# Two attentions computed by pairs of heads in a transformer kernel whose order comes from a planner

## The chip, the cores and the metric

The kernel runs on one core of one Trainium2 chip. What counts is the device time of one execution in microseconds (us). The kernel before takes 2182.76 us, the median of three runs (2174.44 to 2184.56).

## The reference, cut to what matters

Two transformer blocks run one after the other on 512 tokens of width 1024, all in fp32. The first has a gated linear attention and a sliding-window attention side by side, and then a mixture of 16,384 single-neuron experts. The second has a differential attention and a stick-breaking attention side by side, and then a gated feed-forward layer. The change touches the two attentions below. Both have eight heads of 64 channels, so that one head fills half of the 128 rows or columns of TensorE's array.

```python
# sliding window: blocks of 128 queries see their own 128 keys and the 128 before; 8 query heads, 2 key/value heads
sc = jnp.einsum('bnqhgd,bnkhd->bnhgqk', qb, kb) - slopes * dist      # masked
m = jnp.maximum(jnp.max(sc, axis=-1, keepdims=True), sink)
p = jnp.exp(sc - m)
p = p / (jnp.sum(p, axis=-1, keepdims=True) + jnp.exp(sink - m))
o = jnp.einsum('bnhgqk,bnkhd->bnqhgd', p, vb)

# stick-breaking: 8 heads
z = jnp.einsum('bqhd,bkhd->bhqk', qb, k) * scale
log_1mb = jnp.where(mask, jax.nn.log_sigmoid(-z), 0.0)
rem = lax.cumsum(log_1mb, axis=3, reverse=True) - log_1mb
a = jnp.where(mask, jnp.exp(jax.nn.log_sigmoid(z) + rem), 0.0)
return jnp.einsum('bhqk,bkhd->bqhd', a, v)
```

## The kernel before

**A planner writes the order.** The kernel is a set of Python generators, one for each piece of work (the weight streams, each attention, the experts). A small model of the machine (`Model`, L70) keeps the time at which each engine comes free and at which each tile is written; `Meter` (L176) wraps each engine and charges every instruction a cost as it is issued; `Weaver.run` (L253) always steps the generator that could start first, plus a handicap that the generator may ask for with `late`. So the order of instructions on every engine is fixed when the program is built, and follows from the charges. A matmul is charged in one place (L200): a fast price for float32r operands of 256 columns and more, otherwise 1.67 ns for a column, with no regard to what stands beside it.

**Phase one** (L1552) holds the modulation, the input projection of the first block (`w_in`), the gated linear attention (`gla`, L727), the sliding-window attention (`swa`, L886), the output projection, and the first of the expert work. `swa` runs over four blocks of 128 queries. In each it takes the two key/value heads one after the other. The four query heads of one key/value head lie in the same 64 partitions, so the four score matmuls of `scores(kv)` (L902) all use the same half of the array's rows; their results go to two PSUM banks named `b_s`. Then come bias and maximum (VectorE), exponentials (ScalarE), the division, a transpose of the weights, and `values(kv)` (L951): one matmul of 512 columns for each block of keys into the 64 partitions of `b_acc` that belong to this key/value head, that is into one half of the array's columns.

`gla` already alternates: its loop over `i` (L800) puts the lower and the upper 64 rows in turn, and its state update puts the lower and the upper 64 columns in turn.

**Phase two** (L1561) computes the experts of the two middle blocks of tokens densely. The experts of blocks 0 and 3 are done by `sparse` (L1213) in all three phases: GpSimd gathers one row of 1024 numbers for each of 128 tokens by an indirect DMA (`row<-peer_u`, `row<-peer_v`), and VectorE takes it in with one instruction. There are 512 such rows, four in flight, and VectorE does them between its other work.

**Phase three** (L2241) is the second block. `attend` (L1709) is called for tokens 0 to 383 (here called group a) and again for tokens 384 to 511 (group b), which can begin only when `sparse` is through (the key `X3`). It starts two generators, `stick` (L1814) and `diff` (L1894). `stream` (L1620) runs all matmuls with weights for group a: input projections, output projection, then the feed-forward layer in four parts (`b_mm<-u,whi`, `b_mm<-u,wlo`, `b_mm<-fh,whi`, `b_mm<-fh,wlo`), and the projections of group b. The feed-forward layer of group b (`last_feed`, L2137) comes last.

`stick` takes the heads one by one. For a head and a group of key blocks, `front` (L1817) computes scores into one of two PSUM banks `b_z` from 64 rows of the array (`b_z<-mix,sk`), ScalarE makes three passes over them, VectorE makes the log terms `L`; `back` (L1851) adds the cumulative sums by matmuls with a triangular matrix (`b_z<-L,tri`, `b_z<-Ss,tri`, `b_z<-hide,identb`, all 128 rows), ScalarE takes the exponential into `sba`, and a matmul with the values fills 64 columns (`b_osb<-sba,sv`). The loop puts the front of the next unit ahead of the back of this one:

```python
yield from front(*units[0])
for i, (h, g) in enumerate(units):
    if i + 1 < len(units):
        ...
        yield from front(*units[i + 1])
    yield from back(h, g)
```

Group a has 16 units (eight heads, two groups of key blocks of 384 columns each), group b has eight (512 columns).

The functions that the change touches stand here, with the line numbers that the profile uses; every record in the profile carries L224, the line of `Meter` that issues the instruction, so work is told apart by the names of tiles.

Of the kernel before, what the change touches and what calls it, by code (L numbers as in the profile page):

```python
# [9 lines left out]
F32 = mybir.dt.float32  # L10
# [59 lines left out]
class Model:  # L70
# [7 lines left out]
    def __init__(self):  # L78
        self.free = dict.fromkeys(self.ENGINES, 0.0)
        self.cells = {}  # L80
        self.slots = {}
        self.count = {}
        self.shapes = {}
        self.busy = []
        self.last = 0.0
        self.table = None
        self.tick = [0, 0.0, 0.0]

# [87 lines left out]
class Meter:  # L176
# [7 lines left out]
    def __getattr__(self, op):  # L184
# [5 lines left out]
        def call(*args, **kw):  # L190
# [97 lines left out]
def _emit(ctx, tc, A, dbg):  # L288
# [597 lines left out]
    def swa(pa):  # L886
        for b in range(4):
# [22 lines left out]
            def largest(kv, pss):  # L910
                hs = slice(4 * kv, 4 * kv + 4)
                s = S[kv] = pa.tile([128, 4, 256], F32, name="ss", bufs=2)
                for j in range(4):
                    h = 4 * kv + j
                    DVE.tensor_tensor_reduce(s[:, j, k0:], pss[j // 2][:, j % 2, k0:], dist[:, k0:], 2.0 ** -(h + 1),
                                             -3.0e38, OP.add, OP.max, mx[:, h:h + 1])
                tt(mx[:, hs], mx[:, hs], sinks[:, hs], OP.max)
                tt(es[:, hs], sinks[:, hs], mx[:, hs], OP.subtract)
                DVE.tensor_scalar(mx[:, hs], mx[:, hs], -1.0, None, op0=OP.mult)

            def exps(kv):
                hs = slice(4 * kv, 4 * kv + 4)
                s = S[kv]
                act(es[:, hs], es[:, hs], AF.Exp)
                for j in range(4):
                    h = 4 * kv + j
                    act(s[:, j, k0:], s[:, j, k0:], AF.Exp, bias=mx[:, h:h + 1], accum_out=sm[:, h:h + 1])

            def scale(kv):
                hs = slice(4 * kv, 4 * kv + 4)  # L930
                s = S[kv]
                tt(sm[:, hs], sm[:, hs], es[:, hs], OP.add)
                DVE.reciprocal(sm[:, hs], sm[:, hs])
                tt(s[:, :, k0:], s[:, :, k0:], sm[:, hs][:, :, None].to_broadcast([128, 4, 128 * nk]), OP.mult)

            def turn(kv):
                s = S.pop(kv)
# [771 lines left out]
    def attend(b0, b1, u, tag, pair):  # L1709
# [104 lines left out]
        def stick():  # L1814
            Z, L, po, later, now = {}, {}, {}, {}, {}
# [537 lines left out]
```

## Time and profile before

| | us |
|---|---|
| median of three runs | 2182.76 |
| the profiled execution | 2181.23 |
| its span, first to last instruction | 2179.5 |
| TensorE busy in it | 1987.3 (91%) |
| VectorE busy in it | 1796.9 (82%) |
| ScalarE busy in it | 964.6 (44%) |
| GpSimd busy in it | 662.3 (30%) |
| granted TensorE clock, mean | 0.963 of full speed |

1.7 us of the profiled execution lie outside its span. An fp32 matmul appears as two records on PE, so two records of 256 columns are one matmul of 256 columns. The end of a record is modelled; starts are measured, and the distance from the start of a run of records to the start of what follows is the safest measure of what the run took.

### The profile page before, as it was taken

The page shows a single profiled execution, that of the slowest core. Times are in us where ns is not written, and L with a number is a line of the kernel's source. Part 1 is how long each engine was busy: PE and PEld are TensorE (multiplying, and loading weights), DVE is VectorE, ACT ScalarE, POOL GpSimd, SP SyncE. Part 2 cuts the span into 40 slices and gives each one's busy share as a digit, 9 for nine tenths or more (in the row PEclk, how much of TensorE's full clock was granted, in tenths as well). Part 3 has the DMA queues.
Part 4 walks back from the last instruction along what each step waited for, and adds up shares of the span by engine and source line. Part 5 has one row for each costly group of instructions (what it writes and reads, how often), then busy time and mean ns, then how long its engine had stood idle before and what let it go on. Part 6 is the DMA issues. An engine that isn't in the chain of part 4 may idle for free.

```text
span 2179.5 us, 33115 instructions
## 1 busy us (share of the span) xinstructions
PE 1987.3 (91%) x11701; PEld 1748.8 (80%) x11701; DVE 1796.9 (82%) x3731; ACT 964.6 (44%) x1802; POOL 662.3 (30%) x523
## 2 busy tenths in 40 slices
PE   2889799698999977999999999789988999999998
PEld 1778677587889865799999898578767999988987
DVE  7845887879999977899898798889899999844587
ACT  1331442212586533444444544455554333445365
POOL 0000223432212234454444243345443655300000
PEclk9899899699999988999999999999999999999999
DMA  9964447898888999999999899878876999953487
GB/s 368 354 213 130 151 131 224 261 352 307 297 303 305 329 330 353 339 393 373 385 352 363 305 401 344 301 265 300 290 237 203 371 374 369 331 165 106 165 309 262
DMA packets 226453, 638.11 MB, mean 293 GB/s; under 512 B 21056, under 2 KB 70608, under 8 KB 226288
## 3 DMA queue, kind: packets, MB, share of 16 engines
q1 hardware_dynamic: 152560, 367.54, 47.7%
q0 software_dynamic: 73728, 268.47, 34.5%
q8 instruction: 92, 1.51, 0.3%
q14 instruction: 73, 0.60, 0.1%
HBM read 611.54 MB, written 24.38 MB: 292 GB/s over the span
## 4 chain that ended last, share of the span: by engine, by line
PE 49%; DVE 21%; DMA 13%; issue 9%; POOL 5%; ACT 2%; SPq 0%; DVEq 0%; POOLq 0%; ACTq 0%
PE b_mm L224 31%; PE b_dacc L224 8%; POOL row L224 5%; PE b_z L224 4%; DMA row<-peer_v,eU 4%; DVE row L224 3%; PE b_w L224 3%; DVE o L224 3%; DVE vacc L224 3%; DMA wraw<-peer_v 3%; DVE wlo L224 2%; DMA row<-w_ada 1%; PE b_osb L224 1%; DMA aR<-act_d 1%; DMA row<-w_up 1%
## 5 line engine op out<-in xcount | busy, mean ns | idle before, releaser
L224 POOL DMA_INDIRECT row<-peer_u,eU x256 | 329.4, 1287 | 784.4 <-DVE row L224 247.9
L224 POOL DMA_INDIRECT row<-peer_v,eU x256 | 330.0, 1289 | 436.4 <-DVE row L224 197.8
L224 PE MATMUL b_mm<-h,whi 128*128 128x256 f32 (+2 forms) x1648 | 332.4, 296 | 2.7 <-ACT whi L224 2.2
L224 DVE SCALAR_TENSOR_TENSOR vacc<-row,dots,vacc 128x1024 f32<-128x1024 f32 x254 | 325.4, 1281 | 6.9 <-DMA row<-peer_v,eU 6.3
L224 PE MATMUL b_mm<-u,whi 128*128 128x384 f32 x1216 | 324.2, 347 | 7.5 <-DVE mix L224 2.9
L224 DVE SCALAR_TENSOR_TENSOR row<-row,h2n 128x1024 f32<-128x1024 f32 x256 | 310.6, 1219 | 8.3 <-DMA row<-peer_u,eU 8.2
L224 PEld LDWEIGHTS b_mm<-h,whi 128*128 128x128 f32 (+1 forms) x1648 | 271.9, 190 | 24.0 <-issue 6.9
L224 PE MATMUL b_mm<-h,wlo 128*128 128x256 f32 (+2 forms) x824 | 242.8, 295 | 13.9 <-DVE wlo L224 13.9
L224 PEld LDWEIGHTS b_mm<-u,whi 128*128 128x128 f32 x1216 | 219.1, 190 | 24.8 <-issue 5.6
L224 ACT ACTIVATE whi<-wraw 128x1024 fp32r<-128x1024 f32 (+3 forms) x129 | 125.3, 972 | 184.4 <-PE b_mm L224 126.9
L224 PE MATMUL b_mm<-u,wlo 128*128 128x384 f32 x608 | 205.3, 338 | 0.4 <-DVE wlo L224 0.4
L224 ACT ACTIVATE vhi<-wraw 128x1024 fp32r<-128x1024 f32 x128 | 135.6, 1061 | 146.3 <-PE b_dacc L224 75.4
L224 PE MATMUL b_dacc<-vhi,ghi 128*128 128x512 f32 x512 | 165.3, 405 | 27.7 <-ACT ghi L224 27.5
L224 PE MATMUL b_mm<-h,uraw 128*128 128x256 f32 x704 | 166.3, 385 | 4.5 <-DMA uraw<-peer_uT 3.1
L224 PEld LDWEIGHTS b_mm<-h,wlo 128*128 128x128 f32 (+1 forms) x824 | 156.4, 190 | 16.0 <-DVE wlo L224 15.0
L224 PE MATMUL b_dacc<-vlo,ghi 128*128 128x512 f32 x512 | 163.0, 400 | 1.4 <-DVE vlo L224 1.4
L224 PE MATMUL b_dacc<-vhi,glo 128*128 128x512 f32 x512 | 160.9, 395 | 0.0
L224 DVE TENSOR_TENSOR vlo<-wraw,vhi 128x1024 fp32r<-128x1024 f32 x128 | 156.3, 1221 | 1.8 <-PE b_dacc L224 1.8
L224 PEld LDWEIGHTS b_mm<-h,uraw 128*128 128x128 f32 x704 | 131.7, 194 | 21.2 <-issue 3.5
L224 DVE TENSOR_TENSOR wlo<-wraw,whi 128x1024 fp32r<-128x1024 f32 (+3 forms) x129 | 143.6, 1114 | 3.1 <-ACT whi L224 2.3
L224 DVE TENSOR_TENSOR wlo<-uraw,whi 128x1024 fp32r<-128x1024 f32 x84 | 103.0, 1226 | 44.9 <-ACT whi L224 44.9
L224 PEld LDWEIGHTS b_dacc<-vhi,ghi 128*128 128x128 f32 x512 | 91.9, 192 | 48.0 <-ACT ghi L224 34.0
(376 smaller groups left out, 3696.2 us busy)
## 6 DMA issues: line engine op xcount, KB each, us to landing
uraw<-peer_uT SPq DMA_DIRECT2D x128, 512.0 KB, 6.7
wraw<-peer_v SPq DMA_DIRECT2D x128, 512.0 KB, 8.2
wraw<-w_in SPq DMA_DIRECT2D x60, 512.0 KB, 6.1
row<-w_ada SPq DMA_DIRECT2D x48, 512.0 KB, 7.5
wraw<-w_peer_q SPq DMA_DIRECT2D x32, 512.0 KB, 6.4
gt<-gate_d SPq DMA_DIRECT2D x16, 1024.0 KB, 12.2
gate_d<-stg SPq DMA_DIRECT2D x16, 896.0 KB, 7.4
row<-w_in SPq DMA_DIRECT2D x24, 512.0 KB, 4.3
```

Of the source, the lines that this page charges most:

```text
L224: return f(*args, **kw)
```

## The change

Three things change. `Meter` prices matmuls anew: bfloat16 operands get the fast price, and a matmul that uses 64 rows or 64 columns is charged 0.01 us if the matmul issued just before it used the other half. `swa` no longer goes by key/value heads: a step `u` takes two query heads of each key/value head, the score matmuls alternate between the halves of the rows (and between the two banks), and `values(u)` alternates between the halves of the columns with 256 columns each. `stick` takes a pair of heads at once: both banks `b_z` hold one pair, fronts and value matmuls alternate between the halves, and the front of the next unit is issued after the back of this one.

```diff
             elif op in ("matmul", "transpose"):
                 n = math.prod(args[2].shape[1:]) if op == "matmul" else 128
-                fast = args[1].dtype == F32R and n >= 256
-                m.run("PE", n * 0.000417 + 0.013 if fast else max(n, 32) * (0.00167 if op == "matmul" else 0.00083) + 0.01, [out],
-                      rest,
-                      rows=args[1].shape[0])
+                fast = args[1].dtype == F32R and n >= 256 or args[1].dtype == BF
+                cost = n * 0.000417 + 0.013 if fast else max(n, 32) * (0.00167 if op == "matmul" else 0.00083) + 0.01
+
+                first = lambda ap: ap.offset // math.prod(list(ap.tensor.shape)[1:])
+                k, c = args[1].shape[0], math.prod(args[1].shape[1:])
+                part = ("rows", first(args[1])) if k == 64 else ("columns", first(out)) if c == 64 else None
+                beside = part and m.part and part[0] == m.part[0] and part[1] != m.part[1]
+                m.part = None if beside else part
+                m.run("PE", 0.01 if beside else cost, [out], rest, rows=args[1].shape[0])
...
-            def scores(kv):
-                r = slice(64 * kv, 64 * kv + 64)
+            def scores(u):
                 pss = [bank("s").rearrange("p (j k) -> p j k", j=2) for _ in range(2)]
-                for j in range(4):
-                    PE.matmul(pss[j // 2][:, j % 2, k0:], qs[r, j, 128 * b:128 * b + 128],
-                              ks[r, 128 * b - 128 + k0:128 * b + 128], start=True, stop=True)
+                for i in range(2):
+                    for kv in range(2):
+                        r = slice(64 * kv, 64 * kv + 64)
+                        PE.matmul(pss[kv][:, i, k0:], qs[r, 2 * u + i, 128 * b:128 * b + 128],
+                                  ks[r, 128 * b - 128 + k0:128 * b + 128], start=True, stop=True)
                 return pss
...
-            def values(kv, pTs):
-                r = slice(64 * kv, 64 * kv + 64)
+            def values(u, pTs):
                 for kb, pT in enumerate(pTs, 2 - nk):
-                    PE.matmul(po[r, :], vs[:, b - 1 + kb, 64 * kv:64 * kv + 64], pT, start=(kb == 2 - nk),
-                              stop=(kb == 1))
+                    for kv in range(2):
+                        PE.matmul(po[64 * kv:64 * kv + 64, 256 * u:256 * u + 256],
+                                  vs[:, b - 1 + kb, 64 * kv:64 * kv + 64], pT[:, 256 * kv:256 * kv + 256],
+                                  start=(kb == 2 - nk), stop=(kb == 1), skip_group_check=True)
...
-            def front(h, g):
-                j, r = h // 2, slice(64 * (h % 2), 64 * (h % 2) + 64)
+            def front(j, g):
                 jbs, w = groups[g]
-                z = Z[h, g] = bank("z")
+                zs = Z[j, g] = [bank("z") for _ in half]
                 for jb in jbs:
                     o, m = offs[jb]
-                    PE.matmul(z[:, o:o + m], sk[r, j, 128 * jb:128 * jb + 128], sq[r, j, q0(jb) - c0:],
-                              start=(jb == jbs[0]), stop=True, skip_group_check=True)
+                    for z, r in zip(zs, half):
+                        PE.matmul(z[:, o:o + m], sk[r, j, 128 * jb:128 * jb + 128], sq[r, j, q0(jb) - c0:],
+                                  start=(jb == jbs[0]), stop=True, skip_group_check=True)
...
-                    PE.matmul(po[j][r, n - m:n], sv[:, jb, 64 * h:64 * h + 64], a[:, o:o + m],
-                              start=(jb == b1 - 1), stop=(jb == 0), skip_group_check=True)
...
+                    for i, r in enumerate(half):
+                        PE.matmul(po[r, n - m:n], sv[:, jb, 128 * j + 64 * i:128 * j + 64 * i + 64],
+                                  as_[i][:, o:o + m], start=(jb == b1 - 1), stop=(jb == 0), skip_group_check=True)
...
-            units = [(h, g) for h in range(8) for g in range(len(groups))]
...
+            for j in range(4):
+                for q in ("sq", "sk", "sv"):
+                    yield need(f"{q}{j}{tag}")
+                for g in range(len(groups)):
+                    yield from front(j, g)
+                    if g == 0:
+                        po = bank("osb")
+                    yield from back(j, g, po)
+                yield from unit_norm(sq[:, j], po[:, :n], col("gsb"), "w", False)
+                W.set(f"stick{j}{tag}")
```

Three places show how the order moves. The first is PE in phase one, the second block of queries of the sliding window: transposes `b_s`, values `b_acc`, and the input projection `b_mm<-h` between them. Before:

```order
L224 MATMUL b_acc<-pTs,vs 64x512 x2
L224 MATMUL b_s<-ident,ss 128x128 x8
L224 MATMUL b_mm<-h_141,whi 128x384 x2
L224 MATMUL b_mm<-h_141,wlo 128x384
L224 MATMUL b_mm<-h_141,whi 128x384 x2
L224 MATMUL b_mm<-h_141,wlo 128x384
L224 MATMUL b_acc<-pTs,vs 64x512 x2
```

And after:

```order
L230 MATMUL b_acc<-pTs,vs 64x256 x4
L230 MATMUL b_s<-ident,ss 128x128 x8
L230 MATMUL b_mm<-h_141,whi 128x384 x2
L230 MATMUL b_mm<-h_141,wlo 128x384
L230 MATMUL b_mm<-h_141,whi 128x384 x2
L230 MATMUL b_mm<-h_141,wlo 128x384
L230 MATMUL b_acc<-pTs,vs 64x256 x4
```

The places stay; two matmuls of 512 columns in one half of the columns have become four of 256 that alternate between the halves.

The second is PE in phase three, stick-breaking of group a: the first values `b_osb` of a head, the fronts `b_z<-mix,sk`, the stream `b_mm<-u` and pieces of the differential attention (`b_w`, `b_odf`). Before:

```order
L224 MATMUL b_w<-dk,mix 128x256 x2
L224 MATMUL b_osb<-sba,sv 64x128
L224 MATMUL b_osb<-sba,sv 64x256
L224 MATMUL b_z<-mix,sk 128x128
L224 MATMUL b_z<-mix,sk 128x256
L224 MATMUL b_mm<-u,whi 128x384 x2
L224 MATMUL b_mm<-u,wlo 128x384
```

And after:

```order
L230 MATMUL b_osb<-sba,sv 64x128 x2
L230 MATMUL b_osb<-sba,sv 64x256 x2
L230 MATMUL b_w<-ident,dp 128x128
L230 MATMUL b_mm<-u,whi 128x384 x2
L230 MATMUL b_mm<-u,wlo 128x384
L230 MATMUL b_mm<-u,whi 128x384 x2
L230 MATMUL b_mm<-u,wlo 128x384
L230 MATMUL b_z<-mix,sk 128x384 x2
```

Before, the values of one head stand next to the scores of another; now both heads of a pair stand together, and the next front follows only after their values.

The third is PE where group b begins: the first `b_mm<-u,row` is the first projection of group b. Before:

```order
L224 MATMUL b_mm<-u,whi 128x384 x2
L224 MATMUL b_mm<-u,wlo 128x384
L224 MATMUL b_mm<-u,row 128x128 x16
L224 MATMUL b_mm<-row,u 128x128 x8
L224 MATMUL b_mm<-u,row 128x128 x8
L224 MATMUL b_z<-mix,sk 128x128 x4
L224 MATMUL b_mm<-u,row 128x128 x8
L224 MATMUL b_z<-mix,sk 128x128 x4
```

And after:

```order
L230 MATMUL b_mm<-fh,whi 128x384 x2
L230 MATMUL b_mm<-fh,wlo 128x384
L230 MATMUL b_mm<-u,row 128x128 x16
L230 MATMUL b_mm<-row,u 128x128 x8
L230 MATMUL b_mm<-u,row 128x128 x8
L230 MATMUL b_z<-mix,sk 128x128 x8
L230 MATMUL b_mm<-u,row 128x128 x8
L230 MATMUL b_mm<-row,u 128x128 x8
```

The stream of group a stands further on when group b begins. Counted over the whole order, 2112 of its matmuls stood ahead of group b's first projection, 201 between that and the matmuls by which `last_feed` takes in the residual, and 39 behind; now 2247, 105 and none. On VectorE, 406 of the 512 rows of `sparse` stood ahead of the last output of the differential attention of group a, and 395 do now; ahead of the first `glo` of the dense experts in phase two it was 134 and is 130, ahead of phase two's end 314 and 311.

## Rows read from the trace of the kernel before

**Rows 1.** The page's first part: busy us, share of the span, instructions.

```profile
span 2179.5 us, 33115 instructions
PE 1987.3 (91%) x11701; PEld 1748.8 (80%) x11701; DVE 1796.9 (82%) x3731; ACT 964.6 (44%) x1802; POOL 662.3 (30%) x523
```

**Rows 2.** Busy us by stage: stretch, its length, each engine, PEclk, DMA share, GB/s.

```profile
243.00:326.00 83.00, 78.92 (x481) 62.37 (x480) 70.45 (x169) 36.19 (x85) 26.78 (x23) 0.96 0.52 174
424.00:780.00 356.00, 337.10 (x1960) 305.51 (x1960) 323.43 (x1168) 177.59 (x426) 94.21 (x86) 0.96 0.89 314
905.00:1408.00 503.00, 497.99 (x3101) 445.17 (x3099) 449.28 (x600) 243.75 (x369) 210.96 (x149) 1.00 0.97 359
1450.00:1645.00 195.00, 183.90 (x958) 146.29 (x957) 176.76 (x333) 104.06 (x221) 98.16 (x78) 0.99 0.82 276
1645.00:1909.00 264.00, 252.89 (x1423) 245.72 (x1422) 244.77 (x304) 101.81 (x149) 127.97 (x101) 0.98 0.89 330
1909.00:2060.00 151.00, 148.63 (x1064) 134.71 (x1063) 71.96 (x159) 66.65 (x160) 0.00 (x0) 1.00 0.45 142
2060.00:2180.00 120.00, 108.46 (x726) 97.98 (x724) 86.62 (x92) 75.16 (x89) 0.00 (x0) 0.99 0.80 278
```

**Rows 3.** PE by line, 75 to 330 us: count, busy us, mean ns, idle before.

```profile
L224 PE MATMUL b_s<-ks,yT 64*128 64x256 f32 (+1 forms) x64 | 15.2, 380 | 0.0
L224 PE MATMUL b_acc<-pTs,vs 128*64 128x512 f32 x28 | 13.8, 609 | 0.0
```

**Rows 4.** PE by line, 1450 to 1645 us.

```profile
L224 PE MATMUL b_z<-mix,sk 64*128 64x128 f32 (+2 forms) x48 | 14.6, 411 | 0.0
L224 PE MATMUL b_osb<-sba,sv 128*64 128x128 f32 (+2 forms) x48 | 13.8, 396 | 0.3 <-ACT sba L224 0.2
```

**Rows 5.** PE by line, 1909 to 2060 us.

```profile
L224 PE MATMUL b_z<-mix,sk 64*128 64x128 f32 x64 | 9.2, 285 | 0.0
L224 PE MATMUL b_osb<-sba,sv 128*64 128x128 f32 x64 | 8.7, 279 | 0.0
```

**Rows 6.** PE's timeline at four places: start us, us until the last end, work.

```profile
100.20 0.71 PE L224 MATMUL b_w<-M 64*128 64x128 f32 x8
100.84 1.07 PE L224 MATMUL b_acc<-pTs,vs 128*64 128x512 f32 x2
...
320.03 0.66 PE L224 MATMUL b_w<-vg,M 128*64 128x128 f32 x8
320.52 1.88 PE L224 MATMUL b_acc<-pTs,vs 128*64 128x512 f32 x4
...
1987.39 1.16 PE L224 MATMUL b_z<-mix,sk 64*128 64x128 f32 x8
1988.48 1.60 PE L224 MATMUL b_mm<-u,row 128*128 128x128 f32 x12
...
1991.93 1.02 PE L224 MATMUL b_z<-L,tri 128*128 128x512 f32 x2
...
1998.06 1.09 PE L224 MATMUL b_osb<-sba,sv 128*64 128x128 f32 x8
```

**Rows 7.** The chain of waits, 1660 to 1900 us: start us, us, what.

```profile
1732.91 30.10 PE b_mm L224 x172
```

**Rows 8.** VectorE by line, 1645 to 1893 us: the rows of the sparse experts.

```profile
L224 DVE SCALAR_TENSOR_TENSOR vacc<-row,dots,vacc 128x1024 f32<-128x1024 f32 x85 | 109.1, 1284 | 5.9 <-DMA row<-peer_v,eU 5.3
L224 DVE SCALAR_TENSOR_TENSOR row<-row,h2n 128x1024 f32<-128x1024 f32 x21 | 25.7, 1222 | 0.2 <-DMA row<-peer_u,eU 0.2
```

**Rows 9.** PE's timeline, 1509 us: scores of two attentions that happen to adjoin.

```profile
1509.39 0.59 PE L224 MATMUL b_z<-mix,sk 64*128 64x384 f32 x1
1509.40 0.48 PE L224 MATMUL b_w<-dk,mix 64*128 64x128 f32 x2
```

More of the change, by code (lines that the diff above doesn't have):

```diff
@@ L87, in __init__ @@
         self.tick = [0, 0.0, 0.0]
+        self.part = None
     def pe_cost(self, cost, rows):
@@ L921, in exps @@
[L921 to L934, printed above, removed]
@@ new lines, in exps, with scale @@
+            def exps(u):
+                s = S[u]
+                act(four(es, u), four(es, u), AF.Exp)
+                for i, kv, h in pair:
+                    h += 2 * u
+                    act(s[:, 2 * kv + i, k0:], s[:, 2 * kv + i, k0:], AF.Exp, bias=mx[:, h:h + 1],
+                        accum_out=sm[:, h:h + 1])
+            def scale(u):
+                s = S[u].rearrange("p (k j) q -> p k j q", k=2)[:, :, :, k0:]
+                m = four(sm, u)
+                tt(m, m, four(es, u), OP.add)
+                DVE.reciprocal(m, m)
+                tt(s, s, m[:, :, :, None].to_broadcast([128, 2, 2, 128 * nk]), OP.mult)
@@ L938, in turn @@
+            def turn(u):
+                s = S.pop(u)
                 pts = [bank("s") for _ in range(nk)]
@@ L1838, in front @@
-                run = now.setdefault(h, [])
+                as_ = [pD.tile([128, AW], F32, name="sba", bufs=3)[:, :w] for _ in half]
+                for z, a in zip(zs, as_):
+                    act(a, z[:, :w], AF.Abs)
+                    act(a, a, AF.Exp, scale=-1.0)
+                    act(a, a, AF.Ln, bias=1.0)
+                    yield
+                for i, (z, a) in enumerate(zip(zs, as_)):
+                    l = L[j, i, g] = pD.tile([128, w], F32, name=f"L{g}", bufs=2)
+                    stt(l, z[:, :w], 0.0, a, OP.max, OP.add)
+                    for jb in jbs:
+                        if 128 * jb >= c0:
+                            d = l[:, offs[jb][0]:offs[jb][0] + 128]
+                            tt(d, d, sgt, OP.mult)
+                    run = now.setdefault((j, i), [])
+                    for jb in jbs:
+                        o, m = offs[jb]
+                        later[j, i, jb] = run
+                        new, a0 = [], n - m
+                        for v, a, b in run if jb else ():
+                            t = pD.tile([128, b - a], F32, name="Ss", bufs=2 * max(1, b1 - 2))
+                            tt(t, v, l[:, o + a - a0:o + b - a0], OP.add)
+                            new.append((t, a, b))
+                        e = run[0][1] if run else n
+                        run = ([(l[:, o:o + e - a0], a0, e)] if e > a0 else []) + new
+                    now[j, i] = run
+                    yield
@@ new lines, in back @@
+            def back(j, g, po):
+                jbs, w = groups[g]
+                zs = Z.pop((j, g))
+                kw = dict(start=False, skip_group_check=True)
+                as_ = []
+                for i, z in enumerate(zs):
+                    PE.matmul(z[:, :w], tri[:, 0], L[j, i, g], stop=False, **kw)
+                    for jb in jbs:
+                        o, m = offs[jb]
+                        for v, a, b in later.pop((j, i, jb)):
+                            PE.matmul(z[:, o + m - n + a:o + m - n + b], tri[:, 1], v, stop=False, **kw)
+                        if 128 * jb >= c0:
+                            PE.matmul(z[:, o:o + 128], identb, hide, stop=True, **kw)
+                    yield
+                    as_.append(pD.tile([128, AW], F32, name="sba", bufs=3)[:, :w])
+                    act(as_[i], z[:, :w], AF.Exp)
+                yield
@@ L1878, in stick @@
-            units = [(h, g) for h in range(8) for g in range(len(groups))]
-            for q in ("sq0", "sk0", "sv0"):
-                yield need(q + tag)
+                    for i, r in enumerate(half):
+                        PE.matmul(po[r, n - m:n], sv[:, jb, 128 * j + 64 * i:128 * j + 64 * i + 64],
+                                  as_[i][:, o:o + m], start=(jb == b1 - 1), stop=(jb == 0), skip_group_check=True)
+                yield
             yield need("xn")
             yield need("hide")
-            yield from front(*units[0])
@@ L1884, in stick @@
-            for i, (h, g) in enumerate(units):
-                if i + 1 < len(units):
-                    h2_ = units[i + 1][0]
-                    if h2_ != h and h2_ % 2 == 0:
-                        for q in ("sq", "sk", "sv"):
-                            yield need(f"{q}{h2_ // 2}{tag}")
-                    yield from front(*units[i + 1])
-                yield from back(h, g)
+            for j in range(4):
[8 more added lines that the diff above has]
+                W.set(f"stick{j}{tag}")
```

67 lines of the change are left out of this document (13 added, 54 removed).

## The prediction

> **What bounds the kernel now.** The page comes first: TensorE is busy for 1987.3 of 2179.5 us and VectorE for 1796.9 [rows 1]. An average over stages hides who waits, so the next view is the busy time by stage [rows 2]. Look there for the stages in which PE has no idle time left. From 243 to 326 us, where most of the sliding window runs, PE is busy for 78.9 of 83 us. From 905 to 1408 us it is busy throughout, but the change touches nothing there. From 1450 to 1909 us it is busy for 436.8 of 459 us and from 1909 to 2060 us for 148.6 of 151, with VectorE close behind in the first of these two stretches (421.5 of 459) and far behind in the second (72). A microsecond of PE saved is thus worth nearly one in phase three and something less in the sliding window. From 424 to 780 us VectorE is busy for 323 of 356 us, and what is saved before that stage counts only if VectorE gets through it sooner too.
>
> Next comes the work that is to be paired, by line: 29.0 us of the sliding window [rows 3], 28.4 us of stick-breaking in group a [rows 4], 17.9 us in group b [rows 5], together 75.3 us. The last view is the timeline, and it holds the answer to the main question, whether the array does run two such matmuls at once, because other code in this kernel alternates already [rows 6].
>
> **What a pair costs.** In group b, one head's scores are eight records of 128 columns, all in one half of the rows: from their start to that of the next work pass 1.09 us. The gated linear attention has the same eight records, 64 rows and 128 columns, with the halves in turn: 0.64 us. For columns, its state update with the halves in turn takes 0.49 us for eight records of 128 [rows 6]; the value matmuls of one head in group b, in one half, are eight records with 1.09 us to their last end. So pairs do run side by side on this chip, in rows and in columns. Eight records save 0.45 of 1.09 us, or 41%. The lower bound of the saving is therefore 41%. The upper one comes from longer runs: a pair of heads is 16 records; if all of them cost what one head alone costs, 1.09 us against 2.18, it is 50%. It can exceed that by a little, since a run of half-array work is entered and left once for two heads; 51% is the upper end. I take 48%, near the upper end, since nearly all of the runs here are longer in columns than the one of 0.64 us. The Trainium skill, "TensorEngine Tiling (Array Packing)", section Theoretical Speedup, gives up to twofold for a dimension of 64; the short run above shows 1.7-fold. By the rule the 75.3 us shrink by 37.7 us, by the short run by 31.
>
> **The sum, part by part.** Against the profiled execution, 2181.2 us, of which 1.7 lie outside the span; it is 1.6 us under the median.
>
> *Sliding window.* 29.0 us of pairs, of which the first block of queries (16 records of 128 columns and four of 512, some 4.3 us) runs before 243 us, where PE has slack. Of the other 24.7 us 48% is 11.9 us, inside a stage of 83. VectorE is busy there for 70.5 us, part of it with rows of the sparse experts, which can wait. Its other work in the step (maximum, exponentials, transposes) keeps its count and size. What counts is what gets through the stage from 424 to 780 us, where VectorE is nearly full: the changed order has four fewer sparse rows ahead of the dense experts' first `glo`, at 1.22 us each [rows 8] 4.9 us. I take 6 us, between nothing and 11.9.
>
> *Stick-breaking, group a.* 48% of 28.4 is 13.6 us of PE.
>
> *Stick-breaking, group b.* 48% of 17.9 is 8.6 us, in a stage where PE is the only full engine.
>
> *Where the stream goes.* Phase three ends with group b, which waits for the last of the 512 sparse rows. The changed order puts 135 more stream matmuls ahead of group b. At 0.175 us each (30.10 for 172) [rows 7] that is 23.6 us. If PE sets the moment at which group b begins, it comes 23.6 - 13.6 = 10 us later counted from the start of phase three. If the gathers set it: 11 more rows stand behind the end of group a's attention, and 106 rows took the 248 us from 1645 to 1893 [rows 8], so 11 x 2.34 - 13.6 = 12 us later. The two agree. From there on 96 matmuls fewer stand beside group b (16.8 us) and 39 fewer beside `last_feed` (6.8 us), and the 8.6 us are saved: 32.2 us. Phase three gains 20 to 22 us.
>
> *What is added.* The next pair's front now stands behind this pair's values, and nothing covers the passes on ScalarE and VectorE in between but the stream and the differential attention. In group a's order there is one stretch, after the projections and before the output projection, without any stream matmul; before there was one of like length. In group b the cover shrinks from 201 stream matmuls (35 us) to 105 (18 us). I charge 3 us of PE waiting, between nothing and one uncovered unit (13.7 us, below). Also lost is a chance overlap: in group a some scores of stick-breaking stood beside scores of the differential attention from the other half and began 0.01 us apart [rows 9]; a few tenths of a us each time, at a few places. The bfloat16 price, and the price of pairs in `gla` and `diff`, change no duration, only the order; the DMAs keep their count, and POOL's gathers their order.
>
> Together 20.5 - 3 = 17.5 in phase three and 6 before: 23.5 us, so 2181.2 - 23.5 = 2157.7, say 2157 us.
>
> **Rivals.**
>
> *The banks bind.* Both banks `b_z` belong to one pair, so a next front cannot run during this pair's passes, and stick-breaking becomes a chain. One head's chain in group b, from scores to cumulative sums to values, is 1987.39, 1991.93, 1998.06 [rows 6]: 10.7 us with other work between; I add 3 us for the second head's passes, 13.7 us for a pair. Against it: four pairs are 55 us in a stage of 151, and eight pairs 110 us in group a's 195. For it: in each group the last pair waits for the last projections and then stands alone. If one pair's chain is uncovered in group a and none in group b, 13.7 us are lost in place of the 3 charged: 2168 us; if half of one more is uncovered in group b, 2175. I put it at 2170. The Trainium skill, "TensorEngine Tiling (Array Packing)", section Gotcha 1: PSUM Pressure, says that row tiles need different banks and that pairing raises the pressure on them; the rows show no wait for `b_z` before, as the two banks held two heads in turn.
>
> *Slower: the gathers end later and group b has no cover.* The 11 rows moved behind group a's attention cost 25.7 us where DMA is busy for 89% of the stage [rows 2]. This decides if group a's attention does not end sooner (its end hangs on the last differential units, which the change leaves alone), so that the 13.6 us are not given back, and if group b keeps its 151 us because its chain and not PE sets it. Then 25.7 - 6.8 - 6 = 13 us are lost: 2194 us. Against it: PE is busy in 98% of group b's stage, and a quarter of the stage is the stream of group a (35 us), which has moved.
>
> *It does not do what it says.* The halves alternate in the order, but a wait between the two members (each half of the values needs its own exponential) keeps them from starting together. Then only the order changes: 2181 us. Against it: both members' inputs are complete before either is issued, as the order shows both values behind both cumulative sums.
>
> **How the numbers follow.** The forecast has 0.65, the banks 0.15, slower 0.12, no overlap 0.08. The forecast's own range goes from 41% of the pairs with 8 us of waiting and 3 us in phase one (11 + 3 = 14 us, 2167) to 51% with none and all of phase one (24 + 12 = 36 us, 2145). With the rival of the banks and half of the case without overlap, and a little for the spread of the runs, the range is 2141 to 2180. A measurement of this kernel tells a change from none at about 0.5%, here 11 us: below 2172 is faster, above 2194 slower; the slower rival ends on that line and is counted whole. Faster: 0.65 and half of the banks, 0.72. Same: the other half and no overlap, 0.16. Slower: 0.12.
>
> **What would show it.** The records of `b_z<-mix,sk`, `b_osb<-sba,sv`, `b_s<-ks,yT` and `b_acc<-pTs,vs` should start in twos some hundredths of a us apart or less, and their busy time fall from 75.3 us to some 39. The first projection of group b should come about where it did, less what phase one gives, and the stretch from there to `last_feed` should fall from 151 us to some 128. PE's busy share in both attention stages should stay above 93%; if it falls under that, the banks bind. If group b begins over 20 us later than 1909, the gathers set it, and the forecast is wrong. The dense stage should keep its 503 us.

## The result and the profile after

The changed kernel takes 2157.0 us (median of five runs, 2153.7 to 2160.1) where the kernel before takes 2181.7 beside it (2174.4 to 2184.6). The ratio is 0.9886, 95% interval 0.987 to 0.9902; by the ratio it is 24.9 us faster, 21 to 28. The profiled execution took 2154.1 us. The prediction's rows are answered by these of the changed kernel.

The page's first part, which answers [rows 1]: busy us, share of the span, instructions.

```profile
span 2152.3 us, 33164 instructions
PE 1954.0 (91%) x11721; PEld 1731.5 (80%) x11721; DVE 1784.3 (83%) x3725; ACT 961.8 (45%) x1796; POOL 661.4 (31%) x523
```

PE is busy for 33.3 us less, VectorE for 12.6 less. The stages, with their bounds moved along, answer [rows 2]; the columns are the same.

```profile
234.00:317.00 83.00, 70.52 (x504) 59.14 (x502) 74.23 (x181) 38.85 (x94) 20.17 (x19) 0.96 0.47 154
414.00:770.00 356.00, 334.77 (x1952) 302.47 (x1952) 326.79 (x1182) 174.92 (x419) 99.47 (x90) 0.97 0.91 318
893.00:1396.00 503.00, 498.00 (x3093) 445.53 (x3092) 450.78 (x599) 242.90 (x366) 208.22 (x151) 1.00 0.98 361
1440.00:1629.00 189.00, 176.36 (x988) 146.92 (x987) 168.39 (x321) 106.40 (x225) 85.87 (x69) 0.98 0.79 265
1629.00:1915.00 286.00, 275.83 (x1554) 267.53 (x1554) 266.51 (x332) 110.33 (x161) 145.54 (x113) 0.99 0.89 332
1915.00:2039.00 124.00, 118.54 (x943) 106.53 (x942) 48.09 (x128) 54.13 (x143) 0.00 (x0) 1.00 0.49 157
2039.00:2152.00 113.00, 102.25 (x690) 90.94 (x689) 89.16 (x99) 77.46 (x91) 0.00 (x0) 0.99 0.83 291
```

Look at the second and third lines: the two long stages of phase two kept their length, 356 and 503 us. The stage of the sliding window has lost its limit on PE (70.5 of 83 us, before 78.9) and VectorE is now the busier one. In phase three the stretch of the stream has grown and group b's has shrunk.

The half-array matmuls by line: two rows for the sliding window (75 to 330 us), answering [rows 3]; two for group a (1440 to 1632), answering [rows 4]; two for group b (1919 to 2038), answering [rows 5].

```profile
L230 PE MATMUL b_s<-ks,yT 64*128 64x256 f32 (+1 forms) x64 | 9.1, 406 | 0.0
L230 PE MATMUL b_acc<-pTs,vs 128*64 128x256 f32 x56 | 7.9, 395 | 1.4 <-ACT pTs L230 1.4
...
L230 PE MATMUL b_z<-mix,sk 64*128 64x128 f32 (+2 forms) x48 | 7.6, 409 | 0.0
L230 PE MATMUL b_osb<-sba,sv 128*64 128x128 f32 (+2 forms) x48 | 7.4, 396 | 0.0
...
L230 PE MATMUL b_z<-mix,sk 64*128 64x128 f32 x64 | 4.6, 285 | 0.0
L230 PE MATMUL b_osb<-sba,sv 128*64 128x128 f32 x64 | 4.4, 279 | 0.0
```

The sum is 41.0 us where it was 75.3. The mean of one record has not fallen (285 ns before and after in group b's scores): the overlap shows in the busy time of a group, not in the length of its records. The timeline shows it at one place, a pair's scores in group b; it answers the eight records of one head in [rows 6].

```profile
1926.60 1.16 PE L230 MATMUL b_z<-mix,sk 64*128 64x128 f32 x16
1927.69 2.05 PE L230 MATMUL b_mm<-u,row 128*128 128x128 f32 x16
```

Sixteen records of two heads take the 1.09 us to the next work that eight records of one head took.

Where the 27.2 us between the spans of the two profiled executions came from, by the starts of the same events in both traces (us from the span's start; the end of group a's attention is VectorE's last `mix<-b_odf` of 384 columns):

| event | before | after | later (-: earlier) | step |
|---|---|---|---|---|
| last values of the sliding window | 321.8 | 313.0 | -8.8 | -8.8 |
| first dense `b_dacc` | 780.2 | 770.6 | -9.7 | -0.9 |
| phase three: first `b_mm<-u,whi` | 1421.7 | 1412.0 | -9.7 | 0.0 |
| end of group a's attention | 1644.4 | 1628.3 | -16.2 | -6.5 |
| first projection of group b | 1915.5 | 1919.3 | +3.8 | +20.0 |
| `last_feed` takes in the residual | 2058.5 | 2037.9 | -20.6 | -24.4 |
| end | 2179.5 | 2152.3 | -27.2 | -6.6 |

### The profile page after: what moved, and what is told of

It is laid out like the page before. It is cut to its first block, busy times and chain, and to the rows that moved or that the text cites. A ratio compares the mean times of both kernels' runs of the same rounds, so it can differ in the third digit from the quotient of the medians.

```text
span 2152.3 us, 33164 instructions
## 1 busy us (share of the span) xinstructions
PE 1954.0 (91%) x11721; PEld 1731.5 (80%) x11721; DVE 1784.3 (83%) x3725; ACT 961.8 (45%) x1796; POOL 661.4 (31%) x523
## 4 chain that ended last, share of the span: by engine, by line
PE 50%; DVE 18%; DMA 13%; issue 10%; POOL 5%; ACT 3%; SPq 0%; POOLq 0%; DVEq 0%; ACTq 0%
PE b_mm L230 33%; PE b_dacc L230 8%; POOL row L230 5%; PE b_w L230 4%; DMA row<-peer_v,eU 3%; DVE row L230 3%; PE b_z L230 3%; DVE wlo L230 2%; DMA wraw<-peer_v 2%; DVE vacc L230 2%; DMA row<-w_ada 2%; DVE ti L230 1%; DVE o L230 1%; DMA wraw<-w_in 1%; DMA row<-peer_u,eU 1%
## 5 line engine op out<-in xcount | busy, mean ns | idle before, releaser
L230 PE MATMUL b_mm<-h,whi 128*128 128x256 f32 (+2 forms) x1632 | 327.8, 295 | 4.1 <-ACT whi L230 3.6
L230 PEld LDWEIGHTS b_mm<-h,whi 128*128 128x128 f32 (+1 forms) x1632 | 269.5, 190 | 22.4 <-ACT whi L230 3.8
L230 PEld LDWEIGHTS b_mm<-u,whi 128*128 128x128 f32 x1216 | 219.9, 190 | 22.3 <-issue 4.7
L230 PEld LDWEIGHTS b_mm<-h,wlo 128*128 128x128 f32 (+1 forms) x816 | 154.8, 190 | 14.3 <-DVE wlo L230 13.7
```

Of the source, the lines that this page charges most:

```text
L230: return f(*args, **kw)
```

## The experiments

Each was timed beside the kernel before. "Half-array time" below is added up from the starts of the records of `b_z<-mix,sk` and `b_osb<-sba,sv`, each to the start of the next record on PE, less the time in between in which PE was idle: 42.8 us before (26.0 in group a, 16.8 in group b), 22.3 after (13.8 and 8.5). The expectations below have 43.2 and 22.4, with a little of the idle time counted.

**Parts of the change.** The first is the new prices alone.

```
 kernel before, with in Meter:
+ fast = args[1].dtype == F32R and n >= 256 or args[1].dtype == BF
+ beside = part and m.part and part[0] == m.part[0] and part[1] != m.part[1]
+ m.run("PE", 0.01 if beside else cost, ...)
```

> The kernel before with the new prices of the planner alone: no pair is alternated, only the order of the streams and of the sparse rows changes (in its order 135 more stream matmuls stand ahead of group b, as in the changed kernel, and 9 fewer sparse rows ahead of the end of group a's attention). Theory (the array runs two halves at once, and PE's saved time is the gain): no gain, within 4 us of before, 2178 to 2186 us; group b begins some 20 us later than 1909 and takes some 20 us less, and the busy time of the half-array matmuls stays at 75 us. Rival (the gain is the order: the stream moved ahead of group b): half of the gain or more, 2169 us or less.

Measured: 2182.5 us, ratio 1.0003 (0.9988 to 1.0018). Group b begins at 1937.3 and takes 124.6 us instead of 143.0. So it was the prices, not the pairs, that moved the 135 stream matmuls ahead of group b, and the move by itself is worth nothing that can be measured: it shifts work from one full stage to another.

The second has the pairs and the old prices, the third and fourth one half of the pairs each.

```
 changed kernel, Meter as before:
- m.run("PE", 0.01 if beside else cost, ...)
+ m.run("PE", cost, ...)
```

> The changed kernel with the old prices: all pairs in the code, planned as if each matmul ran alone; 48 stream matmuls fewer than before stand ahead of group b, where the changed kernel has 135 more. Theory (halves at once): busy time of the half-array matmuls 41 us as in the changed kernel, and most of the gain, 2155 to 2165 us; if the stream's place has a worth of its own, it is the difference to 2157, at most some 7 us. Rival (order): 2172 us or more.

> The kernel before with the pairs of the sliding window alone, old prices. Theory: the last values of the window come 8 to 9 us earlier, as in the changed kernel, and 2 to 10 us reach the end: 2172 to 2180 us, since the stick-breaking is untouched. VectorE's stage from 424 to 780 us limits it: if VectorE sets the start of the dense stage, under 4 us reach it. Rival (only the saving in phase three counts; the window's is hidden): no change, 2178 to 2186 us.

> The kernel before with the pairs of stick-breaking alone, old prices. Theory: phases one and two as before (within 2 us), the half-array matmuls of phase three fall from 46 to 24 us busy, phase three gains 12 to 18 us: 2164 to 2170 us. Rival (the banks make stick-breaking a chain, the gain comes from elsewhere): under 6 us, 2176 us or more.

| kernel | us | ratio (95%) | last values | phase three begins | phase three lasts |
|---|---|---|---|---|---|
| before | | | 321.8 | 1421.7 | 757.8 |
| prices alone | 2182.5 | 1.0003 (0.9988 to 1.0018) | 326.1 | 1417.8 | 759.1 |
| window's pairs alone | 2180.1 | 0.9995 (0.9976 to 1.0014) | 319.5 | 1421.4 | 757.2 |
| stick-breaking's pairs alone | 2167.6 | 0.9928 (0.9907 to 0.9948) | 322.1 | 1426.9 | 738.9 |
| all pairs, old prices | 2164.8 | 0.9917 (0.9895 to 0.9939) | 319.5 | 1419.9 | 744.5 |
| changed kernel | 2157.0 | 0.9886 (0.987 to 0.9902) | 313.0 | 1412.0 | 740.3 |

The three columns on the right come from one profile each. Stick-breaking's pairs bring 15.7 us (11 to 20) and the gain lies in phase three, which is 18.9 us shorter in the profile, as the theory has it. The pairs of the sliding window alone bring nothing that can be measured: here the rival ("it is hidden anyway") was right, and the last values came 2.3 us earlier and not 8 to 9. All pairs without the prices are 18.1 us faster, with the prices 24.9; the difference, 6.8 us, is known to some 6 either way.

**Is it the array?** The first edit gave the halves up as an alternating sequence, here shown for stick-breaking's scores, and kept everything else.

```
- for jb in jbs:
-     for z, r in zip(zs, half):
+ for z, r in zip(zs, half):        # one half, then the other
+     for jb in jbs:
          PE.matmul(z[...], sk[r, ...], sq[r, ...])
```

> The changed kernel in which each group of paired matmuls is issued half by half (all of one half, then all of the other) while the planner charges what it charged for the pairs, so the rest of the order stays as it is: the same streams ahead of group b, the same sparse rows, as many entries into half-array work. Theory (the array runs two halves at once): the busy time of these matmuls goes back from 41 us to 68 to 76 us; group b's stretch to the residual grows from 118.6 us by 7 to 9 us; of the some 33 us of PE 15 to 30 reach the end: 2172 to 2187 us. Rival (the gain is the order, or that half-array work is entered half as often): 2165 us or less.

Measured: 2164.1 us, ratio 0.9922 (0.9901 to 0.9943), 7 us slower than the changed kernel. That is below the theory's range and inside the rival's (2165 us or less). The rows by line, group b (1923 to 2046 us), tell why:

```profile
L230 PE MATMUL b_z<-mix,sk 64*128 64x128 f32 x64 | 6.8, 285 | 0.0
L230 PE MATMUL b_osb<-sba,sv 128*64 128x128 f32 x64 | 6.3, 279 | 0.0
```

13.1 us are between the 9.0 of the pairs and the 17.9 of before: the halves still overlapped, without being alternated. The starts of the sixteen records of one pair's scores (four matmuls of one half, two records each, then four of the other) show how:

```
1930.230 1930.444 1930.555 1930.667 1930.779 | 1930.784  (5 ns: the other half's first)
1930.890 1930.998 1931.002 1931.109 1931.114 1931.221 1931.333 ... 1931.668
```

The second half's first record began together with the first half's fifth, while three of the first half were still to come. In group a, with two or four records in a half, next to nothing was lost (14.2 us of half-array time there against 13.8). So the edit did not take away what it was to take away, and it cannot decide for the rival; what it took in group b, 4.1 us of half-array time, appears whole in the stretch from group b's start to `last_feed`, 122.7 us instead of 118.6. (Group a's stretch is 3.8 us longer as well; 2.2 of these are in the same 716 stream matmuls, at a granted clock of 0.97 instead of 0.98.)

The next edit keeps the halves apart in stick-breaking, with a small full-array matmul between them; its control has the same matmuls ahead of each group.

```
+ nc.tensor.matmul(z[:, :32], ident, ident[:, :32], start=True, stop=True)
  # parted: between the halves, which are issued one after the other
  # control: ahead of the alternating group
```

> The changed kernel, and in stick-breaking (the sliding window stays paired) each group of paired matmuls is issued half by half with one small full-array matmul (128 x 128 by 32 columns, into a region that is written over) between the halves: 24 of them; the planner's charges stay as for the pairs. Theory (two halves side by side save the time, and a full-array matmul between them keeps them apart): the half-array matmuls of stick-breaking take 40 to 46 us from start to start in place of 22.4 (43.2 before the change), and the time is 12 to 20 us above the run with the small matmul ahead of each group: 2170 to 2183 us. Rival (the order of the streams is the gain): within 5 us of that run.

> The same 24 small full-array matmuls, here ahead of each group of pairs, which stay as the changed kernel has them: the control for the run with them between the halves. They cost up to 0.3 us each. Both theories: half-array matmuls of stick-breaking 22 to 23 us, time 2157 to 2165 us.

Measured: parted 2186.0 us, ratio 1.0009 (0.9994 to 1.0024); control 2162.1 us, ratio 0.9909 (0.9891 to 0.9927). The difference of 24 us is above the 12 to 20 that were expected, and the parted time above its range. Half-array time 42.7 and 21.6 us. The timeline of a pair's scores in the parted kernel:

```profile
1950.58 1.16 PE L230 MATMUL b_z<-mix,sk 64*128 64x128 f32 x8
1951.67 0.41 PE L1837 MATMUL b_z<-ident 128*128 128x32 f32 x2
1952.01 1.16 PE L230 MATMUL b_z<-mix,sk 64*128 64x128 f32 x8
```

Twice eight records, 1.09 us each to the next, and 0.34 us for the small matmul. The busy time of phases one and two (first line) and of phase three (second) of the parted kernel, and then of the control; the first column behind the stretch's length is PE:

```profile
10.00:1420.00 1410.00, 1262.23 (x7428) 1103.26 (x7429) 1190.05 (x2805) 596.22 (x1153) 410.54 (x321) 0.95 0.85 305
1420.00:2187.00 767.00, 727.47 (x4342) 655.72 (x4340) 595.16 (x915) 361.71 (x640) 248.98 (x195) 0.99 0.76 268
```

```profile
10.00:1410.00 1400.00, 1252.18 (x7428) 1093.69 (x7429) 1188.27 (x2802) 594.03 (x1152) 409.11 (x321) 0.96 0.86 307
1410.00:2154.00 744.00, 704.64 (x4342) 642.79 (x4341) 596.04 (x916) 362.20 (x640) 251.82 (x195) 0.98 0.78 277
```

In phase three the parted kernel has 22.8 us more PE work and is 23 us longer than its control; 21.1 of these are half-array time, and the small matmuls take 8.1 us between the halves where they take 6.4 ahead of the groups. It is 767.6 us long there; less the 8.1 us that is 759.5, what the prices alone have (759.1). Without the overlap nothing of the gain in phase three is left, with the same streams, rows and banks.

The ten us by which its phase three begins later are no effect of the edit. Phases one and two are the same instructions in five of these kernels, and their traces put the last values at 310.5 to 316.8 us, the first `b_dacc` at 768.3 to 776.5 and the start of phase three at 1406.0 to 1420.1, mean 1411.8. So a few us there cannot be read from one profile. The two traces with the order of before have phase three at 1421.7 and 1426.9, mean 1424.3.

**Does VectorE limit the sliding window?** On VectorE 12 rows of the sparse experts stand between 215 us and the window's last values in the changed kernel, 15 before, 18 in the kernel with all pairs and old prices. The edits work on the table that says how late a row may be:

```
- ("gla1", 4.0, None), ("", 6.0, None)
+ ("gla1", 3.0, None), ("", 9.0, None)    # rows out of the window, all pairs, old prices
+ ("gla1", 6.0, None), ("", 6.0, None)    # fewer rows ahead of the dense stage, the same kernel
+ ("gla1", 6.0, None), ("", 8.0, None)    # both, in the changed kernel
```

> Pairs with old prices (2164.8 us), and five of the 13 sparse rows that stood ahead of the sliding window's last unit on VectorE moved behind it; 136 rows instead of 137 stand ahead of the dense experts' first glo, 341 as before ahead of the first row of stick-breaking. Theory (VectorE limits the window, 1.22 us a row): the window's last values come some 6 us earlier than 319.5, about 313.5. What then counts: if VectorE's whole count of rows ahead of the dense stage sets its start, the first dacc stays at 776 us and the time at 2162 to 2167 us; if the window's own end sets it, first dacc comes at about 771 and the time falls to 2157 to 2161 us. Rival (PE limits the window in spite of the pairs): last values stay at 319 us.

> Pairs with old prices, the same 13 sparse rows ahead of the window's last unit, but 130 instead of 137 ahead of the dense experts' first glo (the changed kernel has 130), and nine more in the stage of group a's attention. Theory (the rows that VectorE must do ahead of the dense stage set its start): the window's last values stay at 319.5, the first dacc comes 6 to 8.5 us earlier than 776.3, at about 769; group a's attention ends up to 11 us later in turn (nine rows at 1.22 us), so that the end is 2157 to 2166 us. Rival (the window's own end sets it): first dacc at 775 or later.

> The changed kernel with sparse rows put off by two numbers of the pacing table: 7 instead of 10 ahead of the sliding window's last unit, 122 instead of 130 ahead of the dense experts' first glo, 325 instead of 332 ahead of stick-breaking, 391 instead of 395 ahead of the end of group a's attention. Theory (VectorE's rows ahead of the dense stage set its start, 1.22 us each, and the stream stage has room for them): last values 2 to 4 us earlier than 313, first dacc 5 to 10 us earlier than 770.6, of which 0 to 4 are given back in group a (three rows more inside it): 2148 to 2156 us. Rival (what is put off is waited for later): 2157 us or more.

The rows by line, with all pairs and old prices (215 to 319.5 us), and with five rows moved out (215 to 312.3 us):

```profile
L225 DVE SCALAR_TENSOR_TENSOR row<-row,h2n 128x1024 f32<-128x1024 f32 x18 | 21.6, 1216 | 5.3 <-DMA row<-peer_u,eU 5.2
```

```profile
L225 DVE SCALAR_TENSOR_TENSOR row<-row,h2n 128x1024 f32<-128x1024 f32 x11 | 13.3, 1217 | 3.6 <-DMA row<-peer_u,eU 3.6
```

With seven fewer by the trace, the last values came at 312.3 us, 7.2 earlier: with 18 rows ahead (three traces, last values at 319.5, 319.5 and 323.0), VectorE does set the end of the paired window. But the rows then stood behind it, the queries of the experts (first `b_mm<-h,wraw`) began 5.6 us later instead of earlier, the first `b_dacc` came at 784.2 instead of 776.3, and the whole took 2173.7 us (ratio 0.9962, 0.9945 to 0.9978): neither number that was expected. The second edit gave 2173.6 us (0.9965, 0.9952 to 0.9979), missing its range as well: first `b_dacc` 3.9 us earlier, inside the spread named above, and group a's attention 13.7 us longer (227.4 us, PE waiting for 20.9 of them instead of 12.9) with the nine rows it had got. The third gave 2156.9 us, ratio 0.9883 (0.9862 to 0.9905), the changed kernel's own time, outside the theory's range: first `b_dacc` 769.1, phase three at 1412.2. Its last values came at 312.8 us and not 2 to 4 us before 313. The busy time from 215 us to the last values, of the changed kernel with 12 rows and of this one with 9 (the third column is VectorE):

```profile
215.00:313.00 98.00, 80.82 (x526) 64.93 (x528) 90.88 (x278) 46.07 (x112) 18.49 (x18) 0.91 0.40 133
```

```profile
215.00:312.80 97.80, 81.02 (x536) 66.17 (x536) 83.65 (x235) 45.15 (x110) 15.33 (x15) 0.91 0.36 116
```

VectorE had 14 us to spare there instead of 7, and the window ended no sooner. So VectorE's rows set its end with 18 of them ahead, and no longer with 12. That the rows set the start of the dense stage is not borne out.

**What keeps half of group a's saving?** Two edits, one against VectorE, one against the banks:

```
- ("dv3a", 1.0, "DVE")
+ ("mixa", 1.0, "DVE"), ("dv3a", 8.0, "DVE")     # no rows in group a's second half
```

```
  # in back(), ahead of this pair's values:
+ if ahead and all operands of the next pair are there:
+     yield from begin(*ahead)                   # the next pair's scores
```

> The changed kernel with 16 sparse rows moved from the second half of group a's attention behind its end (379 instead of 395 ahead of it). Theory (VectorE, and not the banks, kept half of group a's saving): PE's 6 us of waiting between 1572 and 1590 us go down to 2 or less, and group a's differential attention ends 5 to 8 us earlier than 1628, at about 1621 to 1623. Rival (the two banks b_z make stick-breaking a chain there): its end moves by under 2 us. In either case the 16 rows (19.5 us of VectorE) stand in a stage where VectorE is busy for 268 of 287 us already, so the end is 2152 to 2165 us.

> The changed kernel with the next pair's scores issued right after this pair's last exponential and ahead of its values, wherever their operands are there (most of group a, nothing in group b). Theory (the waits of some 7 us in the second half of group a are the chain of the differential attention): group a's stretch stays at 216 us within 3, and the time at 2153 to 2161 us. Rival (the two banks b_z make stick-breaking the chain there): the stretch falls by 4 to 8 us and the time to 2149 to 2154 us.

The first held back far more than meant: with "DVE" in the entry a row comes 8 us later than whatever else VectorE could do, and 133 rows waited until the stream was over. The time, 2401.2 us (ratio 1.1002, 1.0979 to 1.1025), says nothing about group a; its trace does. The stretch 1550 to 1632 us of the changed kernel, and 1550 to 1625 of this one:

```profile
1550.00:1632.00 82.00, 72.76 (x397) 57.73 (x397) 72.08 (x149) 47.92 (x106) 28.55 (x26) 0.96 0.70 227
```

```profile
1550.00:1625.00 75.00, 65.53 (x354) 51.18 (x354) 47.04 (x114) 42.66 (x93) 5.99 (x7) 0.95 0.37 115
```

VectorE's share fell from 88 to 63%, and PE waited as long as in the changed kernel: 9.2 and 9.5 us. Group a's stretch from the start of phase three was 215.5 us instead of 216.2, with 14.8 us of PE waiting instead of 14.5. So VectorE's load is not the cause. The early scores gave 2165.0 us (ratio 0.9913, 0.9891 to 0.9935), slower if anything, and a stretch of 222.5 us. The rival's gain did not come, and the theory's own range was missed too; as the edit moves the scores and adds no bank, it does not settle what the banks cost. PE's granted clock was 0.94 from 1440 to 1634 us there, 0.98 in the changed kernel from 1440 to 1629. Worked out from these rows as an estimate: at the lower of the two levels, 1.2 GHz, for 12 and 4% of the stretch, that is some 8 us of work lost. What brought the clock down in that run is open; a wait of 3.1 us of PE that the changed kernel does not have stands in it.

The runs of the parts say more. The busy time of group a's stretch, from the start of phase three, in the kernel before, with stick-breaking's pairs alone, and in the changed kernel:

```profile
1421.70:1644.40 222.70, 211.02 (x1084) 170.32 (x1083) 198.03 (x366) 117.63 (x245) 113.88 (x91) 0.98 0.83 279
1426.90:1637.90 211.00, 199.03 (x1090) 166.07 (x1089) 193.03 (x361) 118.11 (x245) 112.45 (x88) 0.98 0.84 288
1412.00:1628.30 216.30, 201.82 (x1109) 169.22 (x1107) 190.14 (x358) 119.54 (x246) 103.68 (x83) 0.98 0.80 269
```

The pairs alone, with the same two banks for one pair, shorten the stretch by 11.7 us, as much as their half-array time falls there (11.5), and PE waits for 12.0 us as before (11.7). So neither the pairs nor their banks keep the saving back. What is left is the order under the new prices: 716 stream matmuls instead of 698 stand in the stretch, and PE waits for 14.5 us. With all pairs and the old prices the stretch is 213.7 us, 9.0 shorter. These are single profiles, each good to a few us.

The waits of PE in the changed kernel, 1555 to 1620 us (total, times, longest), name what is late:

```profile
PE b_odf L230 <- ACT daT L230: 4.1, 3, 1.8
PE b_w L230 <- DVE dp L230: 2.9, 2, 1.8
PE b_z L230 <- DVE L L230: 1.3, 2, 0.8
PE b_w L230 <- ACT nr L230: 0.3, 1, 0.3
```

`dp` and `daT` are the differential attention's: 7.0 of 8.6 us, where the kernel before has 4.5 of such waits. Its chain from scores over VectorE and ScalarE to values has nothing beside it there, as the order has no stream matmul between the last projection and the output projection.

## Why the prediction held

The forecast was 2157 us, and the sum behind it 23.5 us against the profiled execution, which gained 27.2: 17.5 in phase three, as summed, and 9.7 ahead of it where 6 were taken. That the median came out at 2157.0 is luck to some us: the sum gave 2157.7, the profiled execution took 2154.1, and the 6 us were a choice between 0 and 11.9 whose reason did not hold. What the runs bear out is the array's overlap and its worth in phase three.

**The pairs.** They start in twos, 7 ns apart, and take 41.0 us where some 39 were expected; 46% saved against 48 taken and a lower bound of 41. By rows, the window saves 41% (29.0 to 17.0 us), group a 47% and group b 50%. The rival that nothing runs side by side is out: keeping the halves apart costs 24 us against its control, 21.1 of them half-array time. The Trainium skill, "TensorEngine Tiling (Array Packing)", section Key Properties, says that tiles operate independently of each other and that only a change of the tiling mode drains the engine. The trace agrees: 5 to 7 ns between records of two halves, but 201 ns from the last half-array record to the small full-array matmul in the parted kernel, against 112 ns from record to record.

**Stick-breaking, group a.** 13.6 us were taken, and its half-array time fell by 12.1. The attention ended 6.5 us earlier in phase three. The rest is accounted for: PE's other work ahead of its end is some 3 us more, with 24 more stream matmuls, and PE waits 2.8 us longer (14.5 instead of 11.7). The first is not lost, only placed elsewhere. With the pairs alone 11.7 us arrived.

**The stream and group b.** Counted from the start of phase three group b begins 13.5 us later, against 10 to 12. Of the 135 stream matmuls 24 stand in group a's stretch and 111 in the next, 19.4 us at the 0.175 of [rows 7], and that stretch grew by 20.0; only 6.5 of the 13.6 us came off ahead of it. Its stretch to `last_feed` was to fall by 16.8 + 8.6 = 25.4 us, to some 128 us; it fell by 24.4, to 118.6. The size was right and the base was not: it fell from the 143 us between these events and not from the 151 between the rows' bounds. The end was to gain 6.8 and gained 6.6.

**Waiting.** Three us were charged; between its records PE waits for 36.1 us in phase three instead of 31.1, so 5. Together phase three gains 17.5 us, the number of the sum.

**The sliding window.** Six were taken between nothing and 11.9. The two profiles show 9.7, the means over repeated traces 12 (five of the changed order, only two of the order before). By the rows, 9.4 us of the 29.0 ran ahead of 243 us and not 4.3, so 19.6 us stood in the stage, and 8.5 of them were saved. The mechanism that the prediction gave, four sparse rows fewer ahead of `glo` in the stage from 424 to 780 us, is not what carried it: that stage kept its 356 us, and putting off more such rows won nothing. The saving was made inside the window, where the changed order has 12 rows instead of 15. In the measured times the window's pairs and the prices bring nothing clear alone, and together, as the changed kernel against stick-breaking's pairs alone, 9.2 us (3 to 15). From 75 us to the last values PE waits 37 to 38 us with the window's pairs and the old prices, 34 in the changed kernel, 32 before. One reason is shown: with the old prices 18 rows stand there, and VectorE sets the paired window's end. What sets it with 12 rows, and why the prices alone bring nothing, is open.

**The rivals.** The mark set for the banks, a busy share under 93% in an attention stage, misled: group a's whole stage has 93%, but its second half 89%, and most of the waits there are the differential attention's. `b_z<-L` accounts for 1.3 us, and with the pairs alone PE waited no longer in the stretch than before. Against the slower rival: group b began 3.8 us later by the clock, not 20, and its cover was enough; where no stream matmul at all stood beside it (the kernel that held the rows back) PE waited for 12.7 us in it instead of 4.4.

## What to carry to other kernels

Look for half-array matmuls in the rows by line and see in the timeline what stands next to them: if the other half's are ready, put both groups together, and count the saving from the group's time, not from a record's. Then ask which engine limits that stage afterwards: in phase three PE did and of 20.5 us saved 17.5 arrived, in the sliding window, under the old order, VectorE did and the pairs alone brought nothing. A planner's new prices can move much work without a gain; run them without the change they belong to, and repeat a trace before reading a few us out of it.

## What the runs showed of the hardware

Alternation is not needed. With all of one half ahead of the other, PE let three records of the first half be pending and began the second half's; runs of two and four records in a half overlapped nearly as well as alternating ones (14.2 against 13.8 us in group a), runs of eight lost about half (12.6 us in group b, between 8.5 and 16.8). One small full-array matmul between the halves, 0.34 us from its start to the next, ended the overlap altogether (42.7 us of half-array time against 21.6 with it ahead of the pair).
